# A scan's 32x32 block inverses put in place on chip instead of through DRAM, with weights and block inputs loaded earlier

## The chip, the cores and the metric

One core of a Trainium2 chip runs the whole program. The metric is the device time of one execution in microseconds, as the median over several runs. The engines are named as in the profile: PE (TensorE, matrix products), DVE (VectorE), ACT (ScalarE), POOL (GpSimd) and SP (SyncE, which here issues every DMA). Each works through its own instructions in order.

## What is computed

One trunk layer of a diffusion backbone over 1152 tokens (128 of context, 1024 latent) of width 1024: a SwiGLU block, a token mixer, a second SwiGLU block, each followed by a layer norm. The mixer projects its input once; one part feeds a bidirectional recurrence, one a pooling branch, one the gates that merge them:

```python
def _rwkv7_step(S, inp):
    r, w, k, v, kk, a = inp
    sa = jnp.einsum('dbhvk,dbhk->dbhv', S, kk)
    S = S * w[..., None, :] - sa[..., :, None] * (kk * a)[..., None, :] + v[..., :, None] * k[..., None, :]
    return S, jnp.einsum('dbhvk,dbhk->dbhv', S, r)
...
u = jnp.einsum('btgc,gcd->btgd', u, p['w_pool']).reshape(b, t, D_B) * p['pool_scale']
y_b = u @ p['w_o_pool']
gate_a = jax.nn.sigmoid(gate_logits[..., :D_MODEL])
gate_b = jax.nn.sigmoid(gate_logits[..., D_MODEL:])
return (gate_a * y_a + gate_b * y_b) @ p['w_out'], s_final
```

There are 16 heads of 64 and two directions.

## The kernel before

**Precision.** Every large product is made of three: a value is split into a high part (a cast) and a low part (the rest), and high x high, high x low, low x high are added in PSUM (`mm3`, lines 155 to 160). So each weight tile is loaded raw (`wr`), cast on ACT (`wh`) and subtracted on POOL or DVE (`wl`). `Weights` (lines 109 to 129) does this by tiles of 1024 columns, `Halves` (lines 131 to 153) by halves of 512 with four buffers of each kind, always with its subtraction on POOL.

**Stages**, in the profile's time: first SwiGLU block and projections up to about 1560 us; a gate phase (lines 888 to 894) in which eight columns of gate logits are computed for three blocks of 384 tokens, with the first two block inverses and the pooling sums beside it; the scan from 1676 us; its end, from 2325 to 2390 us, in which the last group norms are finished; then the output projections and the second SwiGLU block.

**The scan.** The recurrence goes by chunks of 64 tokens: 18 chunks for each of two halves of the heads, 36 steps, each for both directions and eight heads. `main(s)` (line 1090) multiplies the chunk's `ak` with the state (line 1109) and with the masked products `LM` (line 1115) into `xy`; ACT copies this to `Xs` (line 1119); a product with the inverse `W` of a triangular matrix gives `us` (line 1125), which ACT negates into `vu` (line 1128); this updates the state (lines 1135 to 1137) and gives the output `xy`, copied to `yt` (line 1145). Inside the scan all five engines take their instructions in the order in which the program writes them (line 1241).

**The inverses.** A `Solve` (line 749) makes the 64x64 inverses of two step pairs at once: 2 directions x 2 diagonal blocks of 32 x 32 matrices lie on 128 partitions, 32x32 elements each. `pairs` eliminates row after row on DVE (lines 772 to 779). The result `Wd` has the matrix on the partition and its row and column along it; the matmuls need the row (or column) on the partition. `out` therefore stores it to DRAM, `back` loads it in pieces of 32 elements into `Wb` and `Dx`, and `t0` and `t1` transpose 32x32 blocks on DVE. `ph1` and `ph2` then make the off-diagonal block on PE, with ACT copies between. The work of a solve is spread over 24 slots, three in each scan step (`at`, line 828): slot 0 is after the Xs copies, slot 1 after the vu copies, slot 2 at the end of a step. Solve i + 1 starts 12 slots after solve i, and its loads of `Gq` (line 765) are issued in the slot in which solve i stores `Wd`. There are nine solves; seven store their result in the scan.

**The filler.** Between the scan's products PE gets the remaining gate projections and the pooling branch (`filler`, line 956), one matmul at a time: for each of three blocks of tokens eight `proj` (24 matmuls each, two halves of weights), four pooling products and eight `back` (12 matmuls, one half). `fill` (line 1215) deals out 780 of some 900 of these over the 36 steps in the proportion 6 : 9 : 10 for the three slots. `Halves.get(i)` casts the halves up to i + 2 and has one more fetched. Blocks 1 and 2 read their inputs `hg` back from DRAM (line 1002); the pooled inputs `uf` are loaded by `load_u` (line 992) into two buffers.

**SP's queue** carries all of this in program order: chunk loads (line 867) three steps ahead, `vu` (line 875), the solve's loads and stores, weights (line 140), block inputs, and the stores collected by `later` and issued by `flush`.

Of the kernel before, what the change touches and what calls it, by code (L numbers as in the profile page):

```python
# [9 lines left out]
F32 = mybir.dt.float32  # L10
# [7 lines left out]
P = 128  # L18
# [43 lines left out]
def tile_step(ctx: ExitStack, tc: tile.TileContext, I: dict, O: dict):  # L62
# [68 lines left out]
    class Halves:  # L131
# [11 lines left out]
        def get(self, i, look=2):  # L143
            while len(self.got) < min(len(self.units), i + 1 + look):
                self.fetch(len(self.got) + 1)
                r = self.raws[len(self.got)]
                h = self.pool.tile([P, self.HW], F32R, name="wh", tag="wh", bufs=4)
                l = self.pool.tile([P, self.HW], F32R, name="wl", tag="wl", bufs=4)
                A.copy(h, r)  # L149
                G.tensor_tensor(l, r, h.bitcast(F32), ALU.subtract)  # L150
                self.got.append((h, l))
            self.fetch(len(self.got) + 1)
            return self.got[i]
# [443 lines left out]
    with pool("mp", 4, psum=True) as psum, pool("ma", 2, psum=True) as paux, \  # L597
# [151 lines left out]
        class Solve:  # L749
# [30 lines left out]

            def out(self):
                self.pairs(31)
                self.ed = dram.tile([2, 2, 32, 32, 32], F32, name="ed", tag="ed", bufs=2)
                S.dma_start(self.ed.rearrange("d b n i t -> (d b n) i t"), self.Wd)

            def back(self):
                W = self.W = Wb[self.i % 2]
                self.D = self.t4("Dx", "dx")
                self.N = self.t4("Nt", "nt")
                for b in range(2):  # L790
                    S.dma_start(W[32 * b:32 * b + 32, :, 32 * b:32 * b + 32], self.ed[0, b].rearrange("n i t -> i n t"))
                    S.dma_start(self.D[64 + 32 * b:96 + 32 * b], self.ed[1, b].rearrange("n i t -> i n t"))
                for k in range(2):
                    u = 2 * self.i + k
                    for d in range(2):
                        c0 = chunk0(u, d)
                        S.dma_start(self.N[64 * d:64 * d + 32, k * 16:k * 16 + 16].rearrange("s (a n) t -> s a (n t)", a=4),
                                    nd_d[d][u // 9][c0 // 6][:, :, c0 % 6:c0 % 6 + 2].rearrange("s a c e t -> s a (c e t)"))

            def t0(self):  # L800
                V.transpose(self.D[0:32], self.W[0:32, :, 0:32])

            def t1(self, b):
                r = slice(64 + 32 * b, 96 + 32 * b)
                V.transpose(self.W[r, :, 32 * b:32 * b + 32], self.D[r])

# [7 lines left out]
            def ph1(self, k):  # L814
                ks = slice(16 * k, 16 * k + 16)
                N, D, W = self.N, self.D, self.W
                pm = self.ph(lambda n: ((slice(32, 64), N[0:32, n, :], D[0:32, n, :]), (slice(96, 128), N[64:96, n, :], W[64:96, n, 0:32])), k)
                A.copy(N[32:64, ks], pm[32:64])
                A.copy(N[96:128, ks], pm[96:128])

            def ph2(self, k):
                ks = slice(16 * k, 16 * k + 16)
                N, D, W = self.N, self.D, self.W
                pm = self.ph(lambda n: ((slice(0, 32), N[32:64, n, :], W[32:64, n, 32:64]), (slice(96, 128), D[96:128, n, :], N[96:128, n, :])), k)
                A.mul(W[0:32, ks, 32:64], pm[0:32], -1.0)
                A.mul(W[96:128, ks, 0:32], pm[96:128], -1.0)

            def at(self, n):
# [6 lines left out]
                elif n == 12:  # L835
                    self.out()
                elif n == 14:
                    self.back()
                elif n == 16:
                    self.t0()  # L840
                elif n == 17:
                    self.t1(0)
                elif n == 18:
                    self.ph1(0)
                elif n == 19:
                    self.ph2(0)
                elif n == 20:
                    self.t1(1)
                    self.ph1(1)
                elif n == 21:  # L850
                    self.ph2(1)
# [26 lines left out]
        with pool("m2") as pl:  # L878
# [8 lines left out]
            load_v(1, 0, (2, 17))  # L887
            for n in range(EARLY):
                for b in (2, 1, 0):
                    ps = psum.tile([P, 512], F32, name="pm", tag="mm")  # L890
                    gemm(ps, W.get(27 + n), hs, b)
                    ga = s0.tile([P, 8, 64], F32, name="ga", tag="Xs", bufs=2).rearrange("p h v -> p (h v)")[:, :BN]
                    A.activation(ga, ps[:, :BN], AF.Sigmoid)  # L893
# [34 lines left out]
    for b in range(NB):  # L928
        gunits += [I["w_pool"].rearrange("p g c -> p (g c)"), *halves(mix[39])]
        for n in range(8):  # L930
            if n < 7:
                gunits += halves(mix[40 + n])
            gunits.append(halves(I["w_op"][n // 2])[n % 2])
# [22 lines left out]
    def filler(psG):  # L956
        u = 0

        def nextw(look=2):
            nonlocal u  # L960
            u += 1
            return GW.get(u - 1, look)

        for b in range(NB):
            sl = slice(b * BN, (b + 1) * BN)
            hh = hs[0]
            if b:
                hh = [hpA.tile([P, KT, BN], F32R, name="hg", tag="hb") for k in range(2)]
            if b:
# [28 lines left out]
            wp = nextw()  # L998
            if b:
                for ks in (slice(0, 4), slice(4, 8)):  # L1000
                    for k in range(2):
                        S.dma_start(hh[k][:, ks].bitcast(F32), h2_d[b][k][:, ks])
            first = chain(proj(0), proj(1))
            next(first)
            yield
            for g in range(4):
# [3 lines left out]
                G.tensor_tensor(ul, uf, uh.bitcast(F32), ALU.subtract)  # L1010
                if g < 2:
                    ufs.append(load_u(g + 2))
                for _ in range(PWGAP):
# [3 lines left out]
                yield from steps3(ps[:, :BN], [(w3(wp[0], g), w3(wp[1], g), uh, ul)])  # L1017
                t = sg.tile([P, BN], F32, name="ut", tag="ut")
                A.activation(t, ps[:, :BN], AF.Copy, scale=pcol("pool_scale", g))
                split(t, u2[0], u2[1], g, G)  # L1020
            yield from first
            yield from back(b, u2, gts, 0)
            for n in range(2, 8):
                yield from proj(n)
                if n < 7:
                    yield from back(b, u2, gts, n - 1)
            prev = (b, u2, gts)
# [3 lines left out]
    with pool("s1") as pl, pool("gn") as gn, pool("spa", 2, psum=True) as psA, pool("spx", 1, psum=True) as psX, \  # L1031
# [58 lines left out]
        def main(s):  # L1090
# [7 lines left out]
            LM, KBT = c["LM"].pop(s), c["KBT"].pop(s)  # L1098
            Xs = s0.tile([P, 8, 64], F32, name="Xs", tag="Xs", bufs=2)
            if s % 2 == 0:  # L1100
# [140 lines left out]
        with tc.manual_schedule(engines={PE.engine, V.engine, A.engine, G.engine, S.engine}):  # L1241
# [30 lines left out]
            while gns or waitgn:  # L1272
                if waitgn:
                    gns.append(waitgn.pop(0))
                for _ in range(2):
                    flush()
                    drive(gns)
                    for _ in range(8):
                        next(fl, None)
            for _ in fl:  # L1280
# [179 lines left out]
```

## Time and profile before

| | us |
|---|---|
| median of 3 runs | 3470.34 (3469.39 to 3471.6) |
| the profiled execution, its own time | 3476.58 |
| its span, first to last instruction | 3474.5 |
| PE busy over the span | 3236.0 (93%) |
| DVE busy | 1999.5 (58%) |
| POOL busy | 1311.7 (38%) |
| ACT busy | 1149.4 (33%) |

The profile is that of one execution. Busy shares are over the whole span, and the stages differ: a stage's own limit is read from its windows and from the waits inside it. "Clock" is the share of full speed that was granted to PE. A wait is the idle time of an engine ahead of an instruction, put down to what ended it. L1109 means line 1109 of the kernel before.

### The profile page before, as it was taken

The numbers are of one execution on the slowest core, as the hardware profiler recorded it, in microseconds if no ns is written. First come the engines' busy times: TensorE is split into PE (matmuls) and PEld (weight loads), VectorE is DVE, ScalarE is ACT, GpSimd is POOL, SyncE is SP. The second block draws the span as 40 slices with busy tenths as digits, with TensorE's granted clock in tenths as the row PEclk, the third lists the DMA queues.
The fourth block names the chain that finished last, engine by engine and source line by source line (L and its number), as shares of the span: only waits on it lengthen the run. The fifth ranks groups of instructions, "written<-read, shape, count | busy, mean of one in ns | idle before, by whom it ended". The sixth has DMA issues, their size and how long they took to land.

```text
span 3474.5 us, 62657 instructions
## 1 busy us (share of the span) xinstructions
PE 3236.0 (93%) x25742; PEld 3072.7 (88%) x25742; DVE 1999.5 (58%) x3309; ACT 1149.4 (33%) x1970; POOL 1311.7 (38%) x1026
## 2 busy tenths in 40 slices
PE   7999999999999999798899888988999999999997
PEld 7999999999988887587788777887999999999996
DVE  6888633347557788858476667544574332323466
ACT  4111111125434444431343444454345111111133
POOL 5111211136456666653221442257764111111144
PEclk9999999999999999698999889999999999999998
DMA  6344211124455545564455666656551111111133
GB/s 233 129 140 133 91 37 42 45 92 132 185 167 159 162 151 155 161 194 159 135 159 171 184 178 188 197 160 201 204 168 52 37 42 44 43 43 43 49 127 105
DMA packets 310270, 442.74 MB, mean 127 GB/s; under 512 B 115424, under 2 KB 211168, under 8 KB 308960
## 3 DMA queue, kind: packets, MB, share of 16 engines
q1 hardware_dynamic: 309984, 438.74, 39.8%
q8 instruction: 202, 3.31, 0.4%
q14 instruction: 84, 0.69, 0.1%
HBM read 316.01 MB, written 101.25 MB: 120 GB/s over the span
## 4 chain that ended last, share of the span: by engine, by line
PE 60%; DVE 14%; DMA 10%; issue 5%; POOL 5%; SPq 3%; ACT 3%; DVEq 0%; POOLq 0%; ACTq 0%
PE pg L159 8%; PE pg L160 8%; PE pg L158 8%; PE po L158 5%; PE po L159 5%; PE po L160 5%; PE pm L158 2%; PE pm L160 2%; PE pm L159 2%; PE pa L1078 2%; DVE wl L127 2%; PE xy L1109 2%; DMA fm<-in_w_mod 1%; DVE pr L776 1%; DVE Wd L778 1%
## 5 line engine op out<-in xcount | busy, mean ns | idle before, releaser
L125 ACT CAST wh<-wr 128x1024 fp32r<-128x1024 f32 x270 | 280.7, 1049 | 817.5 <-PE po L159 433.7
L127 POOL TENSOR_TENSOR wl<-wr,wh 128x1024 fp32r<-128x1024 f32 x117 | 291.4, 2490 | 505.7 <-ACT wh L125 473.7
L295 POOL TENSOR_TENSOR gl<-sg,gh 128x384 fp32r<-128x384 f32 x132 | 159.9, 1212 | 783.7 <-ACT gh L294 783.6
L158 PE MATMUL po<-gh,wh 128*128 128x384 f32 x1056 | 357.8, 339 | 6.7 <-DVE acc L312 3.3
L159 PE MATMUL pg<-h1l,wh 128*128 128x384 f32 x1056 | 356.6, 338 | 5.7 <-POOL h1l L167 5.6
L159 PE MATMUL po<-gl,wh 128*128 128x384 f32 x1056 | 357.2, 338 | 3.6 <-POOL gl L295 3.6
L160 PE MATMUL po<-gh,wl 128*128 128x384 f32 x1056 | 358.0, 339 | 0.0
L158 PE MATMUL pg<-h1h,wh 128*128 128x384 f32 x1056 | 357.6, 339 | 0.0
L160 PE MATMUL pg<-h1h,wl 128*128 128x384 f32 x1056 | 355.7, 337 | 0.0
L127 DVE TENSOR_TENSOR wl<-wr,wh 128x1024 fp32r<-128x1024 f32 x153 | 222.7, 1460 | 230.7 <-ACT wh L125 230.7
L158 PE MATMUL pg<-h3h,wh 128*128 128x384 f32 x1056 | 353.6, 336 | 0.0
L160 PE MATMUL pg<-h3h,wl 128*128 128x384 f32 x1056 | 353.3, 335 | 0.0
L159 PE MATMUL pg<-h3l,wh 128*128 128x384 f32 x1056 | 353.1, 335 | 0.0
L158 PE MATMUL pm<-h2h,wh 128*128 128x384 f32 x936 | 329.8, 352 | 12.6 <-ACT ga L893 11.7
L292 DVE TENSOR_TENSOR sg<-sg,pg 128x384 f32<-128x384 f32 x132 | 73.1, 553 | 460.3 <-PE pg L160 454.2
L160 PE MATMUL pm<-h2h,wl 128*128 128x384 f32 x936 | 328.8, 351 | 2.0 <-DVE wl L127 2.0
L159 PE MATMUL pm<-h2l,wh 128*128 128x384 f32 x936 | 328.4, 351 | 0.0
L312 DVE SCALAR_TENSOR_TENSOR ac<-po,modh,ac 128x384 f32<-128x384 f32 (+1 forms) x352 | 172.7, 514 | 96.9 <-PE po L160 96.9
L403 DVE SCALAR_TENSOR_TENSOR fm<-fm 128x512 f32<-128x512 f32 x224 | 182.8, 816 | 53.6 <-DMA fm<-in_w_mod 50.3
L150 POOL TENSOR_TENSOR wl<-wr,wh 128x512 fp32r<-128x512 f32 x75 | 98.5, 1316 | 303.9 <-ACT wh L149 223.8
L158 PEld LDWEIGHTS po<-gh,wh 128*128 128x128 f32 x1056 | 199.5, 189 | 9.6 <-PE po L160 3.6
L159 PEld LDWEIGHTS pg<-h1l,wh 128*128 128x128 f32 x1056 | 200.5, 190 | 8.1 <-POOL h1l L167 7.6
(285 smaller groups left out, 7565.3 us busy)
## 6 DMA issues: line engine op xcount, KB each, us to landing
wr<-in_ffn_in SPq DMA_DIRECT2D x120, 512.0 KB
ak<-ak SPq DMA_DIRECT2D x48, 768.0 KB
ak<-ak SPq DMA_DIRECT2D x72, 512.0 KB
wr<-in_ffn_out SPq DMA_DIRECT2D x60, 512.0 KB
fm<-in_w_mod SPq DMA_DIRECT2D x112, 256.0 KB
wr<-in_w_mix SPq DMA_DIRECT2D x39, 512.0 KB
sh<-pads SPq DMA_DIRECT2D x108, 130.0 KB
wr<-in_w_mix SPq DMA_DIRECT2D x48, 256.0 KB
```

The source lines that it names most:

```text
L125: A.copy(h[:, :w], r[:, :w])
L127: e.tensor_tensor(l[:, :w], r[:, :w], h[:, :w].bitcast(F32), ALU.subtract)
L150: G.tensor_tensor(l, r, h.bitcast(F32), ALU.subtract)
L158: PE.matmul(ps, wh, xh, start=first and k == 0, stop=False)
L159: PE.matmul(ps, wh, xl, start=False, stop=False)
L160: PE.matmul(ps, wl, xh, start=False, stop=last and k == n - 1)
L292: lastv[0] = V.tensor_tensor(sg, sg, pu[:, :BN], ALU.mult)
L295: G.tensor_tensor(gs[j, b][1][:, sl], sg, gs[j, b][0][:, sl].bitcast(F32), ALU.subtract)
L312: lastv[0] = V.scalar_tensor_tensor(accs[b][:, n, s0:s1], po[:, s0:s1], modh[:, gate_i // 4, n, g:g + 1], accs[b][:, n, s0:s1], ALU.mult, ...
L403: V.scalar_tensor_tensor(jk, w, 1.0, silc[:, s, hf * 512:hf * 512 + 512], ALU.mult, ALU.mult, accum_out=part[:, kt, s, hf:hf + 1])
L1078: PE.matmul(pa[e][:, i, :], ak[es, i, 128:256], ak[es, i, 0:128], start=True, stop=True)
L1109: PE.matmul(xy[:, e, d, i, :], ak[d][es, i, 0:128], states[q, d][es, i, :], start=(i == 0 and d == 0), stop=False, skip_group_check=True)
```

## The change

The solve keeps its result on chip: two DVE transposes over all 128 partitions make `X` (row on the partition) and `Y` (column on the partition), and four ACT copies (two per direction, in two slots) put the diagonal blocks into `W`. The products of `ph1` and `ph2` come one slot earlier for the first half. `Halves.get` fetches two halves beyond the cast ones instead of one. A block's inputs `hg` are loaded after the last projection of the block before, ahead of three `back` groups, and each `back` comes one projection later; the order of the weight halves follows. `uf` is scaled in place, and its buffer's next load follows the split. In the gate phase two weight columns go together, and block 0's products of both come last; its results have buffers of their own. In the end of the scan one drive of the group norms and ten filler matmuls make a round instead of two drives with eight each.

```diff
--- before.py
+++ after.py
@@ -149,7 +149,7 @@
                 A.copy(h, r)
                 G.tensor_tensor(l, r, h.bitcast(F32), ALU.subtract)
                 self.got.append((h, l))
-            self.fetch(len(self.got) + 1)
+            self.fetch(len(self.got) + 2)
             return self.got[i]
 
     def mm3(ps, pairs, first=True, last=True):
@@ -778,18 +778,16 @@
                     V.tensor_tensor(Wd[:, 0:k + 1, k + 1:32], Wd[:, 0:k + 1, k + 1:32], o, ALU.subtract)
                 self.k = min(31, self.k + n)
 
-            def out(self):
+            def swap(self):
                 self.pairs(31)
-                self.ed = dram.tile([2, 2, 32, 32, 32], F32, name="ed", tag="ed", bufs=2)
-                S.dma_start(self.ed.rearrange("d b n i t -> (d b n) i t"), self.Wd)
+                Wd = self.Wd
+                self.X = self.t4("Xi", "dx")
+                self.Y = self.t4("Yt", "yt")
+                V.transpose(self.X.rearrange("p n t -> p t n"), Wd.rearrange("p i t -> p t i"))
+                V.transpose(self.Y.rearrange("p n i -> p i n"), Wd)
 
             def back(self):
-                W = self.W = Wb[self.i % 2]
-                self.D = self.t4("Dx", "dx")
                 self.N = self.t4("Nt", "nt")
-                for b in range(2):
-                    S.dma_start(W[32 * b:32 * b + 32, :, 32 * b:32 * b + 32], self.ed[0, b].rearrange("n i t -> i n t"))
-                    S.dma_start(self.D[64 + 32 * b:96 + 32 * b], self.ed[1, b].rearrange("n i t -> i n t"))
                 for k in range(2):
                     u = 2 * self.i + k
                     for d in range(2):
@@ -797,12 +795,11 @@
                         S.dma_start(self.N[64 * d:64 * d + 32, k * 16:k * 16 + 16].rearrange("s (a n) t -> s a (n t)", a=4),
                                     nd_d[d][u // 9][c0 // 6][:, :, c0 % 6:c0 % 6 + 2].rearrange("s a c e t -> s a (c e t)"))
 
-            def t0(self):
-                V.transpose(self.D[0:32], self.W[0:32, :, 0:32])
-
-            def t1(self, b):
-                r = slice(64 + 32 * b, 96 + 32 * b)
-                V.transpose(self.W[r, :, 32 * b:32 * b + 32], self.D[r])
+            def place(self, d):
+                W = self.W = Wb[self.i % 2]
+                for b in range(2):
+                    r = slice(64 * d + 32 * b, 64 * d + 32 * b + 32)
+                    A.copy(W[r, :, 32 * b:32 * b + 32], (self.Y if d else self.X)[r])
 
             def ph(self, jobs, k):
                 pm = PPS[0].tile([P, 16, 32], F32, name="ph", tag=PPS[1])
@@ -813,15 +810,15 @@
 
             def ph1(self, k):
                 ks = slice(16 * k, 16 * k + 16)
-                N, D, W = self.N, self.D, self.W
-                pm = self.ph(lambda n: ((slice(32, 64), N[0:32, n, :], D[0:32, n, :]), (slice(96, 128), N[64:96, n, :], W[64:96, n, 0:32])), k)
+                N, W, Y = self.N, self.W, self.Y
+                pm = self.ph(lambda n: ((slice(32, 64), N[0:32, n, :], Y[0:32, n, :]), (slice(96, 128), N[64:96, n, :], W[64:96, n, 0:32])), k)
                 A.copy(N[32:64, ks], pm[32:64])
                 A.copy(N[96:128, ks], pm[96:128])
 
             def ph2(self, k):
                 ks = slice(16 * k, 16 * k + 16)
-                N, D, W = self.N, self.D, self.W
-                pm = self.ph(lambda n: ((slice(0, 32), N[32:64, n, :], W[32:64, n, 32:64]), (slice(96, 128), D[96:128, n, :], N[96:128, n, :])), k)
+                N, X, W = self.N, self.X, self.W
+                pm = self.ph(lambda n: ((slice(0, 32), N[32:64, n, :], W[32:64, n, 32:64]), (slice(96, 128), X[96:128, n, :], N[96:128, n, :])), k)
                 A.mul(W[0:32, ks, 32:64], pm[0:32], -1.0)
                 A.mul(W[96:128, ks, 0:32], pm[96:128], -1.0)
 
@@ -833,19 +830,17 @@
                 elif n < 12:
                     self.pairs((2, 1, 5)[n % 3])
                 elif n == 12:
-                    self.out()
-                elif n == 14:
+                    self.swap()
+                elif n == 13:
                     self.back()
-                elif n == 16:
-                    self.t0()
+                    self.place(0)
+                elif n == 15:
+                    self.place(1)
                 elif n == 17:
-                    self.t1(0)
+                    self.ph1(0)
                 elif n == 18:
-                    self.ph1(0)
-                elif n == 19:
                     self.ph2(0)
                 elif n == 20:
-                    self.t1(1)
                     self.ph1(1)
                 elif n == 21:
                     self.ph2(1)
@@ -885,11 +880,11 @@
                 load_ak(s_, cs_, 0)
             load_v(0, 0, (0, 1))
             load_v(1, 0, (2, 17))
-            for n in range(EARLY):
-                for b in (2, 1, 0):
+            for n0 in range(0, EARLY, 2):
+                for n, b in ((n0, 2), (n0, 1), (n0 + 1, 2), (n0 + 1, 1), (n0, 0), (n0 + 1, 0)):
                     ps = psum.tile([P, 512], F32, name="pm", tag="mm")
                     gemm(ps, W.get(27 + n), hs, b)
-                    ga = s0.tile([P, 8, 64], F32, name="ga", tag="Xs", bufs=2).rearrange("p h v -> p (h v)")[:, :BN]
+                    ga = pl.tile([P, 8, 64], F32, name="ga", tag="ga", bufs=2).rearrange("p h v -> p (h v)")[:, :BN]
                     A.activation(ga, ps[:, :BN], AF.Sigmoid)
                     S.dma_start(gab_d[n][b][:, 0, :], ga)
             for g, w in enumerate(WINDOWS):
@@ -927,9 +922,10 @@
 
     for b in range(NB):
         gunits += [I["w_pool"].rearrange("p g c -> p (g c)"), *halves(mix[39])]
+        gunits += halves(mix[40])
         for n in range(8):
-            if n < 7:
-                gunits += halves(mix[40 + n])
+            if n < 6:
+                gunits += halves(mix[41 + n])
             gunits.append(halves(I["w_op"][n // 2])[n % 2])
     BO = (1, 0, 2)
     GW = Halves(gctx.enter_context(pool("gw", side="right")), gunits)
@@ -961,11 +957,9 @@
             u += 1
             return GW.get(u - 1, look)
 
+        hh = hs[0]
         for b in range(NB):
             sl = slice(b * BN, (b + 1) * BN)
-            hh = hs[0]
-            if b:
-                hh = [hpA.tile([P, KT, BN], F32R, name="hg", tag="hb") for k in range(2)]
             if b:
                 for n in (6, 7):
                     yield from back(*prev, n)
@@ -996,10 +990,6 @@
 
             ufs = [load_u(0), load_u(1)]
             wp = nextw()
-            if b:
-                for ks in (slice(0, 4), slice(4, 8)):
-                    for k in range(2):
-                        S.dma_start(hh[k][:, ks].bitcast(F32), h2_d[b][k][:, ks])
             first = chain(proj(0), proj(1))
             next(first)
             yield
@@ -1008,22 +998,24 @@
                 uh, ul = [sg.tile([P, BN], F32R, name="us", tag=f"us{k}", bufs=1) for k in range(2)]
                 A.copy(uh, uf)
                 G.tensor_tensor(ul, uf, uh.bitcast(F32), ALU.subtract)
-                if g < 2:
-                    ufs.append(load_u(g + 2))
                 for _ in range(PWGAP):
                     next(first)
                     yield
                 ps = psG.tile([P, 512], F32, name="pw", tag="mm")
                 yield from steps3(ps[:, :BN], [(w3(wp[0], g), w3(wp[1], g), uh, ul)])
-                t = sg.tile([P, BN], F32, name="ut", tag="ut")
-                A.activation(t, ps[:, :BN], AF.Copy, scale=pcol("pool_scale", g))
-                split(t, u2[0], u2[1], g, G)
+                A.activation(uf, ps[:, :BN], AF.Copy, scale=pcol("pool_scale", g))
+                split(uf, u2[0], u2[1], g, G)
+                if g < 2:
+                    ufs.append(load_u(g + 2))
             yield from first
-            yield from back(b, u2, gts, 0)
             for n in range(2, 8):
                 yield from proj(n)
-                if n < 7:
-                    yield from back(b, u2, gts, n - 1)
+                if n == 7 and b < 2:
+                    hh = [hpA.tile([P, KT, BN], F32R, name="hg", tag="hb") for k in range(2)]
+                    for ks in (slice(0, 4), slice(4, 8)):
+                        for k in range(2):
+                            S.dma_start(hh[k][:, ks].bitcast(F32), h2_d[b + 1][k][:, ks])
+                yield from back(b, u2, gts, n - 2)
             prev = (b, u2, gts)
         for n in (6, 7):
             yield from back(*prev, n)
@@ -1096,7 +1088,7 @@
             vu = [vus[d][u % 2][:, m[d]] for d in range(2)]
             ak = aks.pop(s)
             LM, KBT = c["LM"].pop(s), c["KBT"].pop(s)
-            Xs = s0.tile([P, 8, 64], F32, name="Xs", tag="Xs", bufs=2)
+            Xs = s0.tile([P, 8, 64], F32, name="Xs", tag="Xs", bufs=1)
             if s % 2 == 0:
                 c["yt"] = pl.tile([P, 2, 8, 64], F32, name="yt", tag="yt", bufs=1)
             yt = c["yt"]
@@ -1272,11 +1264,10 @@
             while gns or waitgn:
                 if waitgn:
                     gns.append(waitgn.pop(0))
-                for _ in range(2):
-                    flush()
-                    drive(gns)
-                    for _ in range(8):
-                        next(fl, None)
+                flush()
+                drive(gns)
+                for _ in range(10):
+                    next(fl, None)
             for _ in fl:
                 pass
             flush()
```

## Rows read from the trace of the kernel before

**Rows 1.** Windows: busy us (instructions) of PE, PEld, DVE, ACT, POOL; clock; DMA. Last: L1109 alone.
```profile
1707.00:2261.00 554.00, 489.01 (x8689) 440.00 (x8690) 373.36 (x755) 247.97 (x458) 161.60 (x132) 0.91 0.61 178
...
2325.00:2390.00 65.00, 39.24 (x181) 34.96 (x179) 23.35 (x35) 24.17 (x49) 42.13 (x33) 0.82 0.61 195
...
1707.00:2261.00 554.00, 66.67 (x962) 62.33 (x964) 0.91 0.61 178
```

**Rows 2.** Windows, the same columns: the first of four steps without a stall; their sum.
```profile
2107.30:2125.20 17.90, 17.64 (x421) 16.05 (x420) 14.59 (x30) 11.07 (x21) 5.73 (x6) 1.00 0.57 173
...
sum 61.90, PE 61.55 PEld 55.67 DVE 49.20 ACT 31.30 POOL 14.72; mean PE 15.39 PEld 13.92 DVE 12.30 ACT 7.82 POOL 3.68
```

**Rows 3.** Waits of PE, 1676 to 2261 us: total us, times, longest.
```profile
PE us L1125 <- ACT Xs L1119: 15.3, 4, 7.9
...
PE pm L940 <- ACT wh L149: 12.9, 1, 12.9
...
PE pm L940 <- DMA hg<-h: 10.6, 2, 7.9
...
PE sp L1135 <- ACT vu L1128: 8.9, 2, 5.6
...
PE xy L1109 <- ACT yt L1145: 8.5, 2, 6.8
...
PE xy L1109 <- POOL Sc L1046: 4.3, 1, 4.3
...
PE pm L942 <- DMA hg<-h: 2.6, 2, 1.4
...
PE pm L940 <- ACT ut L1019: 1.3, 1, 1.3
```

**Rows 4.** Waits of ACT, the same stretch and columns.
```profile
ACT wh L149 <- DMA wr<-in_w_mix: 54.1, 8, 14.0
...
ACT wh L149 <- DMA wr<-in_w_op: 27.3, 7, 5.9
```

**Rows 5.** Timeline of SP's DMA issues, 1985 to 2030 us: start, us, what.
```profile
1991.08 7.71 SPq L765 DMA_DIRECT2D Gq<-qd  x8
...
2000.77 0.61 SPq L140 DMA_DIRECT2D wr<-in_w_mix  x1
```

**Rows 6.** Timeline of ACT and PE, same stretch; in brackets the idle time before.
```profile
2009.26 0.62 ACT L149 CAST wh<-wr 128x512 fp32r<-128x512 f32 x1 [14.03 <-DMA wr<-in_w_mix]
...
2010.26 1.18 ACT L1119 COPY Xs<-xy 64x512 f32<-64x512 f32 x2
...
2010.89 1.41 PE L1125 MATMUL us<-Xs,Wb 64*64 64x64 f32 x12 [7.87 <-ACT Xs L1119]
```

**Rows 7.** Solve's operations: ns min/median/max, first and last start us; page: DMA packets.
```profile
L791 SPq DMA_DIRECT2D Wb<-ed x18: 318/617/4921, 1596.4 to 2225.7; - x18
...
L792 SPq DMA_DIRECT2D Dx<-ed x18: 546/564/4314, 1596.8 to 2226.3; - x18
...
L805 DVE STREAM_TRANSPOSE Wb<-Dx x18: 1235/1239/1242, 1602.0 to 2259.1; 32x1024 f32<-32x1024 f32 x18
...
L825 ACT ACTIVATE Wb<-ph x18: 587/588/591, 1613.5 to 2266.2; 32x512 f32<-32x512 f32 x18
...
DMA packets 310270, 442.74 MB, mean 127 GB/s; under 512 B 115424, under 2 KB 211168, under 8 KB 308960
```

**Rows 8.** Timeline of DVE: first and last pair product of one solve.
```profile
1558.31 0.19 DVE L776 TENSOR_TENSOR pr<-Wd,Gq 128x31 f32<-128x31 f32 x1 [6.99 <-DMA Nt<-nd]
...
1592.10 0.23 DVE L778 TENSOR_TENSOR Wd<-Wd,pr 128x31 f32<-128x31 f32 x1
```

**Rows 9.** Waits of the SP queue, 1676 to 2261 us: total us, times, longest.
```profile
SPq L994 <- POOL us L1010: 26.3, 5, 10.7
```

**Rows 10.** Waits of PE in the gate phase, 1560 to 1676 us.
```profile
PE pm L158 <- ACT ga L893: 11.7, 1, 11.7
...
PE ph L811 <- DVE Dx L801: 4.9, 1, 4.9
```

## The prediction

> **What bounds the kernel now.** I read the busy table by stretch first, then TensorE's waits in the scan, then ScalarE's waits, and last the SP queue and ScalarE side by side in one bad stretch. [...] Four steps without a stall (one of them with the inverse's matmuls) take 61.9 us, 61.55 busy, the first at clock 1.00 [rows 2]. The stretch holds 962/32 = 30 steps [rows 1], so stall-free it would last 30/4 x 61.9 = 464 us. It lasts 554: 90 us too many, 65 idle and about 25 of work slowed by the clock, which falls after such idle times. TensorE itself therefore bounds the scan, wherever nothing interrupts it.
>
> TensorE's waits from step 0 on name the interrupters: ScalarE's copies Xs, vu and yt, with 15.3, 8.9 and 8.5 us, a memset of the state on POOL with 4.3, together 37.0; the block inputs `hg` from DRAM with 10.6 + 2.6 = 13.2; and 12.9 once, for the first weights of the filler [rows 3]. The small copies are not slow; they queue. In the same stretch ScalarE stood 54.1 + 27.3 us idle ahead of its weight casts of line 149, waiting for the weights to land [rows 4]. One stretch shows the whole chain: SP takes 7.7 us to issue the eight `Gq` loads of the next solve and issues a weight load only at 2000.77 [rows 5]; the cast comes at 2009.26 after 14.03 us of waiting; Xs sits behind it on the in-order ScalarE at 2010.26, and TensorE resumes at 2010.89 after 7.87 us [rows 6]. So late DMA, behind the solve's loads in one queue, becomes a TensorE stall.
>
> **The change part by part.**
>
> 1. **One more half of weights ahead.** Today a half is fetched one `get` before the one that casts it, then two. The filler hands out 780 matmuls over 36 steps, 21.7 a step; a half feeds 12. At 61.9/4 = 15.5 us a step [rows 2] a `get` comes every 8.6 us, so each load starts some 8.6 us sooner. Against a longest wait of 14.0 and a mean of 54.1/8 = 6.8 and 27.3/7 = 3.9 us [rows 4], that removes nearly all: beyond 8.6 us only 14.0 leaves more than a few. The extra raw half fits the four buffers: the one it overwrites was cast two `get`s before. I take 85% of the 37.0 us: -31.5. Bounds: 0 (SP as late as before) and -37.
>
> 2. **Block inputs sooner.** The four 768 KB loads go out before three `back` groups, 36 matmuls or 36/21.7 x 15.5 = 26 us sooner; TensorE waited 7.9 us at the longest [rows 3]. I take all 13.2. They now wait for the last projection of the block; what is queued behind them on SP are weights (with their new lead), chunk loads three steps ahead and stores, so nothing that TensorE wants at once.
>
> 3. **The way through DRAM goes.** Per solve this removes one store and four loads. SP issues two of each kind of load, medians 0.62 and 0.56 us, up to 4.9 when the queue is full [rows 7], some 3 to 7 us of queue time per solve. Those loads are 4 x 32 x 32 = 4096 pieces of 128 B per solve, 36,864 of the 115,424 packets under 512 B [rows 7]. The SP wait for `Wd` does not go: the next `Gq` load, right behind it, needs VectorE to be through with the same pairs. I count this as part of step 1's 85%, not again.
>
> 4. **VectorE.** Three transposes of 32x1024 go, 3 x 1.24 = 3.7 us [rows 7]; two of 128x1024 come, in one slot. The trace has none of 128 partitions, and none with the new access patterns, whose neighbouring elements lie 128 B apart. Nearest are the pair products: 31 elements in a row take 0.19 us, 31 single elements 128 B apart 0.23 [rows 8], some 1 ns more per element. From below a transpose costs today's 1.24; from above 1.24 + 1024 x 1 ns = 2.3. I take the upper for both, 4.6 a solve, 0.9 more than today, as rows 8 are nearest in their access pattern [rows 8]. [...] VectorE is busy 49.2 of 61.9 us in the clean steps [rows 2], so I charge nothing; if that cover fails, the state update behind the swap is late, then the next step's transposes of `ak`.
>
> 5. **ScalarE** gets four copies of 32x1024 per solve. A 32x512 pass takes 0.59 [rows 7], so at most 1.2 each, 4.7 a solve, 33 over the seven solves of this stretch. Two sit behind the vu copies, where TensorE has filler, state and output matmuls before it needs ScalarE again; two behind Xs, with filler and the us matmuls. ScalarE is busy 31.3 of 61.9 [rows 2]. Bounds 0 and +33; nearer to 0: I take +4.
>
> 6. **Pool inputs.** `load_u` moves behind the split, so SP waits longer there (today 26.3 us in five waits [rows 9]). The reordered projection and `back` have the same matmuls. Nothing in the sum; it is a rival.
>
> 7. **Gate phase, end.** Two stalls stand before the scan, 11.7 and 4.9 us [rows 10]. The second is the wait for a transpose behind the DRAM trip, but its successor may stand at the same place, and the weights of every second gate column now have one product instead of three in which to be converted. The 11.7 (a store queued on SP) stays. At the end TensorE is busy 39.2 of 65 us [rows 1], paced by POOL; one drive with ten steps instead of two with eight each leaves POOL's work as it was. Both 0, with -17 to +10 as bounds together. The first 12.9 also stays: the first weights are queued behind the same loads.
>
> 8. **Clock.** The addressed idle time is 31.5 + 13.2 = 44.7 of 65; of the 25 us of slow work I give back the same share, -17.
>
> **Sum:** -31.5 - 13.2 - 17 + 4 = -58 us. The profiled execution took 3476.6 us (span 3474.5), 6.2 above the median of 3470.3; the forecast is 3476.6 - 58 = 3418.6 there and **3412** as median. A measurement of this kernel can tell about 0.2%, 7 us.
>
> **Rivals.**
> - *The next limit takes half.* With the weights in time, the copies of step 5 fall on the path (+33 instead of +4): -29, 3441. For it: Xs, vu and yt each hold a step's chain, and they were the longest waits [rows 3]. Against it: ScalarE is half idle in clean steps.
> - *More than forecast.* All 50.2 us of stalls and their 19 of clock go, and the 11.7 + 4.9 of the gate phase [rows 10] with them: -86, 3384. Against it: nothing in the diff moves the first of these.
> - *The lookahead does nothing.* SP itself is late, so a load emitted earlier is still issued behind the same `Gq` loads (7.7 us in a row [rows 5]). Only `hg` and its clock are saved: -18, 3452.
> - *Slower: SP stands still.* Six `load_u` now wait for TensorE, ScalarE twice and POOL in turn, two `hg` groups for a projection. At the longest wait of today, 10.7 us in the same line [rows 9], eight of them cost 86; were all of it TensorE's, -58 + 86 = +28, 3498. It decides from 58/8 = 7.3 us each. Against it: the mean is 26.3/5 = 5.3 [rows 9], and of TensorE's waits only 1.3 us led to this chain [rows 3].
>
> **How the numbers follow.** Forecast (gain of 40 to 80) 0.62; more than that 0.10; half or less 0.15; no change 0.05; slower 0.08. The range 3388 to 3455 holds the forecast, the bounds of its terms and the smaller gains, and leaves out most of "more", "no change" and "slower". Faster 0.87, same 0.05, slower 0.08.
>
> **What would show it.** Right: line 149's waits for weights fall from 81 us in that stretch to under 20, TensorE's waits for `hg` vanish, steps 1 to 30 last under 500 us at a clock of 0.97 or more, packets under 512 B fall by 37 thousand, transposes take 1.2 to 2.3 us. Wrong: line 149 still waits, or Xs and vu wait with the casts in time (step 5), or SP's line 994 waits over 60 us (the slower rival), or the stretch shrinks and the gate phase or the end grows by as much.

## The result, and the profile after

The changed kernel takes 3419.53 us (median of 4 runs, 3412.68 to 3426.26) against 3469.86 us: a ratio of 0.9861, 95% interval 0.9833 to 0.9889, 50 us by the medians. The forecast was 3412, a gain of 58, with a range of 3388 to 3455. The profiled execution took 3418.87 us, where the sum had 3418.6.

The windows of the changed kernel, in the columns of [rows 1]: the gate phase, steps 1 to 30 of the scan, and its end.

```profile
1560.00:1674.00 114.00, 94.65 (x756) 90.95 (x756) 79.52 (x132) 24.67 (x41) 33.65 (x23) 0.88 0.37 128
...
1704.60:2210.80 506.20, 465.09 (x8688) 418.42 (x8687) 372.33 (x743) 280.01 (x488) 162.07 (x131) 0.97 0.58 180
...
2275.00:2334.00 59.00, 39.97 (x179) 35.56 (x178) 23.00 (x33) 24.06 (x49) 43.11 (x33) 0.82 0.65 205
```

The reader is to see that 48 us of the 57.7 between the two profiled executions lie in one stretch, steps 1 to 30 of the scan, 554 to 506 us, with as many products as before. The idle time there fell by 24 us, from 65 to 41; the busy time fell by 24 us too, from 489 to 465, as the granted clock rose from 0.91 to 0.97. The end gave 6 us, the gate phase about 2. The forecast had steps 1 to 30 under 500 us; that was not reached.

What TensorE waited for in the scan (total us, times, longest), to be held against [rows 3] and this line of the same view of the kernel before:

```profile
PE pt L1086 <- DVE Sc L1136: 5.4, 4, 4.2
```

The changed kernel:

```profile
PE pt L1078 <- DVE Sc L1128: 14.5, 11, 2.9
PE pm L936 <- ACT wh L149: 12.8, 1, 12.8
PE sp L1127 <- ACT vu L1120: 11.7, 5, 6.3
PE pw L936 <- DVE gt L983: 6.2, 1, 6.2
PE pb L936 <- DVE gt L983: 3.8, 1, 3.8
PE xy L1101 <- POOL Sc L1038: 2.2, 1, 2.2
```

The waits for `hg`, Xs and yt are gone. VectorE has taken their place: the state update Sc and the gated sums gt, 24.5 us together. The wait for vu did not fall but rose, from 8.9 to 11.7 us. Of ScalarE's 81.4 us of waiting for weights [rows 4] nothing is left, but for the one wait for the first weights:

```profile
ACT wh L149 <- DMA wr<-in_w_pool: 11.4, 1, 11.4
```

The new operations (ns min/median/max), and the page's count of packets, to be held against [rows 7]:

```profile
L786 DVE STREAM_TRANSPOSE Xi<-Wd x9: 2021/2175/2193, 1591.1 to 2172.4; 128x1024 f32<-128x1024 f32 x9
...
L787 DVE STREAM_TRANSPOSE Yt<-Wd x9: 1866/1921/1961, 1593.2 to 2174.5; 128x1024 f32<-128x1024 f32 x9
...
L802 ACT COPY Wb<-Xi x18: 1044/1045/1047, 1593.4 to 2175.7; 32x1024 f32<-32x1024 f32 x18
...
DMA packets 271533, 433.29 MB, mean 127 GB/s; under 512 B 77840, under 2 KB 173584, under 8 KB 270224
```

The transposes take 2.18 and 1.92 us, near the upper bound of 2.3; small packets fell by 37,584.

VectorE's own waits for DMA ahead of line 776, the first pair product of a solve, are still there: 40 us in five groups over steps 1 to 30. The two largest:

```profile
DVE pr L776 <- DMA bb<-bon: 11.7, 1, 11.7
DVE pr L776 <- DMA wr<-in_w_mix: 10.6, 2, 6.1
```

### The profile page after: what moved, and what is told of

Same layout as the page of the kernel before. It is cut to its first block, busy times and chain, and to the rows that moved or that the text cites. A ratio compares the mean times of both kernels' runs of the same rounds, so it can differ in the third digit from the quotient of the medians.

```text
span 3416.8 us, 62644 instructions
## 1 busy us (share of the span) xinstructions
PE 3206.2 (94%) x25742; PEld 3044.4 (89%) x25742; DVE 2002.7 (59%) x3300; ACT 1187.2 (35%) x2006; POOL 1308.0 (38%) x1026
## 4 chain that ended last, share of the span: by engine, by line
PE 60%; DVE 16%; DMA 9%; issue 5%; POOL 5%; ACT 3%; SPq 2%; DVEq 0%; POOLq 0%; ACTq 0%
PE pg L159 9%; PE pg L160 9%; PE pg L158 9%; PE po L159 4%; PE po L158 4%; PE po L160 4%; PE pm L158 2%; PE pm L160 2%; PE pm L159 2%; DVE wl L127 2%; PE pa L1070 2%; PE xy L1101 2%; DVE Wd L778 2%; DVE fm L403 2%; DVE pr L776 2%
## 5 line engine op out<-in xcount | busy, mean ns | idle before, releaser
L160 PE MATMUL pm<-h2h,wl 128*128 128x384 f32 x936 | 328.2, 351 | 16.7 <-DVE wl L127 16.7
L160 PEld LDWEIGHTS pm<-h2h,wl 128*128 128x128 f32 x936 | 182.1, 195 | 24.0 <-DVE wl L127 17.3
```

The source lines that it names most:

```text
L160: PE.matmul(ps, wl, xh, start=False, stop=last and k == n - 1)
```

## The experiments

Theory A is the prediction's: weights that land late stall ScalarE, and through it TensorE. Theory B makes the trip of `Wd` through DRAM the cause, however early the weights are asked for. The first four runs add one part to the kernel before, or take one from the changed kernel. Where a run is held against another one than the kernel before, the difference is that of the two medians; the ratios, each against the kernel before measured beside it, give up to 5 us more or less, and are added where that matters.

**Lookahead alone**, on the kernel before.

```diff
-            self.fetch(len(self.got) + 1)
+            self.fetch(len(self.got) + 2)
             return self.got[i]
```

> The kernel before with the lookahead of two halves and nothing else. Theory A (weights that land late stall ScalarE, and through it TensorE): most of the weight part of the gain, 30 to 45 us faster than before (about 3430 us), ScalarE's waits for weights in line 149 from 112 us in the whole run to under 35. Theory B (the trip through DRAM crowds the queue, and weights are late because of it however early they are asked for): under 12 us faster, line 149 still waits over 70 us.

Measured: 3457.15 us, ratio 0.9977 (0.9956 to 0.9998): 8 us by the ratio. ScalarE's waits in line 149 did what A says, over the whole run:

```profile
ACT wh L149 <- DMA wr<-in_w_pool: 10.5, 1, 10.5
...
ACT wh L149 <- DMA wr<-in_w_mix: 3.0, 2, 2.5
```

From 112 us to 13.5, and yet the time hardly moved: A is right on the waits, B on the time. In steps 1 to 30 TensorE is idle 68 us, no less than before; what this stretch gained came with the clock, 0.94 against 0.91:

```profile
1701.00:2241.50 540.50, 472.69 (x8690) 425.32 (x8688) 373.21 (x755) 248.52 (x457) 161.48 (x131) 0.94 0.63 183
```

The waits for Xs and yt are gone. TensorE's waits from step 1 to 2240 us show what came instead:

```profile
PE pt L1086 <- DVE Sc L1136: 21.5, 7, 6.5
PE pm L940 <- DMA hg<-h: 17.7, 1, 17.7
PE sp L1135 <- ACT vu L1128: 15.4, 2, 9.2
```

The state update on VectorE, with 5.4 us a small row before, is the longest now. One stretch of this kernel shows why, first SP's issues in the timeline (start, us, what):

```profile
1983.92 0.42 SPq L784 DMA_DIRECT2D ed<-Wd  x1
1984.40 7.10 SPq L765 DMA_DIRECT2D Gq<-qd  x8
...
1992.02 0.43 SPq L769 DMA_DIRECT2D Wd<-in_id  x1
```

and VectorE's timeline, with the idle time before an instruction in brackets:

```profile
1998.83 1.26 DVE L776 TENSOR_TENSOR pr<-Wd,Gq 128x31 f32<-128x31 f32 x1 [13.70 <-DMA Wd<-in_id]
...
2010.22 0.41 DVE L1136 TENSOR_TENSOR Sc<-Sc,sp 128x256 f32<-128x256 f32 x1
```

The next solve's `Wd` starts as unit matrices loaded over the old `Wd` (line 769). In SP's queue this load stands behind the store of the old `Wd` and the eight `Gq` loads. VectorE, in order, stands 13.7 us before the first pair product, and the state update of the step stands behind the pairs. Five of TensorE's seven waits for it, 20.4 of the 21.5 us, end 8 to 12 us after such a stand of VectorE has ended.

**On-chip turn alone**, on the kernel before, with what makes room for it.

```diff
-            def out(self): ...
+            def swap(self): ...
-                Xs = s0.tile([P, 8, 64], F32, name="Xs", tag="Xs", bufs=2)
+                Xs = s0.tile([P, 8, 64], F32, name="Xs", tag="Xs", bufs=1)
```

> The kernel before with the transposes and copies on chip, and with what makes room for them (one Xs buffer, pooled inputs scaled in place, gate results in buffers of their own), but with the old lookahead, the old loads of hg, the old order of gate columns and the old end. Theory A: 3 to 15 us faster than before. Theory B: 30 us or more, and line 149's waits for weights fall from 112 us to under 50.

Measured: 3434.95 us, ratio 0.9906 (0.9878 to 0.9933), 33 us by the ratio: theory B in time. Line 149 still waited 72 us, where B had under 50, so B's "because of it" holds only in part.

**Changed kernel without the lookahead.** The edit of the first run, reversed.

> The changed kernel with the old lookahead of one half. Theory A: 25 to 40 us of the gain are lost (about 3450 us), line 149 waits over 70 us for weights. Theory B: under 10 us are lost (about 3425 us).

Measured: 3434.87 us, ratio 0.9906 (0.9881 to 0.9931): 15 us lost, between the two. Line 149 waited 79 us; so the same wait seems to cost more once the trip through DRAM is gone than before, 15 against 8, but the intervals of the two overlap, and this is not shown.

**Changed kernel through DRAM.**

```diff
-            def swap(self): ...
-            def place(self, d): ...
+            def out(self): ...
+            def t0(self): ...
+            def t1(self, b): ...
```

> The changed kernel with the old way of the blocks through DRAM (store, four loads, three transposes of 32 partitions; the old slots). Theory A: 3 to 15 us lost (3422 to 3435 us), with under 30 us of waits for weights in line 149. Theory B: 30 us or more lost (3450 us or more).

Measured: 3450.12 us, ratio 0.9946 (0.9924 to 0.9968): 31 us lost, theory B's number, with 17 us of waits in line 149 as theory A wants it. Late weights were thus one symptom of the queue, and by these medians no more than a third of the gain. VectorE's waits for DMA in this kernel (1700 to 2240 us) are another, 51 us against the 40 of the changed kernel:

```profile
DVE pr L776 <- DMA Wb<-ed: 20.7, 2, 15.0
...
DVE pr L776 <- DMA Wd<-in_id: 12.3, 1, 12.3
DVE pr L776 <- DMA wr<-in_w_mix: 10.9, 1, 10.9
DVE pr L776 <- DMA bb<-bon: 6.7, 1, 6.7
```

All these stand ahead of one and the same line, the first pair product of a solve; the names are those of the transfer that landed last. The next run tests this by taking the unit matrices off the queue.

**Through DRAM, unit matrices on chip** (the run above, with two memsets on POOL).

```diff
-                S.dma_start(self.Wd, I["id32"])
+                G.memset(self.Wd, 0.0)
+                G.memset(self.Wd.rearrange("p i t -> p (i t)")[:, 0:1024:33], 1.0)
```

> The changed kernel with the old way through DRAM, but with the unit matrices made by memsets on POOL: the next solve's start value now waits for the store of the last one alone, not for a load queued behind it. Measured so far: the way through DRAM costs about 30 us (3450 against 3419.5), the load of the unit matrices about 12 without it. If the 30 us are in the main VectorE waiting for that load at the end of the queue: 20 us or more faster than through DRAM with the load (3430 us or less). If they are the queue and the transfers themselves (SP's issue time, small pieces, loads of other work behind them): 5 to 15 us faster, no more than without the trip (3435 to 3445 us).

Measured: 3429.12 us, ratio 0.9895 (0.9879 to 0.9911): 21 us faster than with the load by the medians, 18 by the ratios: about the bound of the first branch. But that branch's reading, that the trip's cost is in the main the wait for this load, does not follow, for the load costs something without the trip too: the same two memsets take 12 us off the changed kernel (below). Putting the trip back costs 31 us with the load and 22 without it (3429 against 3407), so only some 9 of the 31 us hang on the load behind the trip, and the intervals of the four ratios together are wider than that. VectorE still waits 34 us ahead of the pairs here, the largest:

```profile
DVE pr L777 <- DMA y<-y: 11.7, 1, 11.7
DVE pr L777 <- DMA wr<-in_w_mix: 8.4, 1, 8.4
DVE pr L777 <- DMA gab<-gt: 7.2, 1, 7.2
```

**Block inputs late**: the changed kernel with the loads of `hg` where they were.

```diff
+            if b:
+                hh = [hpA.tile([P, KT, BN], F32R, name="hg", tag="hb") for k in range(2)]
...
-                if n == 7 and b < 2:
```

> The changed kernel with the block inputs hg loaded where they were before, behind the first pool inputs of their own block. Step 2 of the prediction: TensorE waits 10 to 20 us for hg again and the time grows by 13 to 20 us (3433 to 3440 us). Rival (the loads are hidden by the shorter queue since the trip through DRAM is gone): under 5 us.

Measured: 3433.35 us, ratio 0.9912 (0.9892 to 0.9931): 14 us lost. TensorE's waits:

```profile
PE pm L936 <- DMA hg<-h: 12.1, 2, 8.9
...
PE pm L938 <- DMA hg<-h: 2.3, 2, 1.2
```

By the ratios it is 18. Step 2 holds: 14.4 us of waits, where the prediction had 13.2 and its share of the clock (5 us).

**ScalarE's copies twice.**

```diff
-                    A.copy(W[r, :, 32 * b:32 * b + 32], (self.Y if d else self.X)[r])
+                    for _ in range(2):
+                        A.copy(W[r, :, 32 * b:32 * b + 32], (self.Y if d else self.X)[r])
```

> The changed kernel with each of the four ScalarE copies of a solve made twice: 4 x 1.04 = 4.2 us more of ScalarE per solve, 38 in all. Step 5 of the prediction (the copies lie beside other work): 0 to 8 us slower. Rival (ScalarE holds the chain of a step): 20 us or more.

Measured: 3428.57 us, ratio 0.9896 (0.9881 to 0.991): 9 us slower by the medians, 12 by the ratios, for 38 us more of ScalarE. Outside the step's bound of 8 and short of the rival's 20: most of the copies are covered, a quarter to a third is not. It shows at vu, 18.1 us where the changed kernel has 11.7:

```profile
PE sp L1128 <- ACT vu L1121: 18.1, 6, 6.6
```

**Transposes twice.**

```diff
-                V.transpose(...)  # both
+                for _ in range(2):
+                    V.transpose(...)  # both
```

> The changed kernel with both transposes made twice: 2.2 + 1.9 = 4.1 us more of VectorE per solve, 37 in all, in the slot of the swap. Step 4 of the prediction (covered by TensorE's work): 0 to 8 us slower. Rival (VectorE holds the state update behind the swap, so TensorE's waits for Sc grow): 20 us or more, waits for Sc from 14 to over 35 us.

Measured: 3445.13 us, ratio 0.9948 (0.9931 to 0.9964): 26 us slower for 37 us more of VectorE (30 by the ratios): the rival. TensorE's waits for the state update doubled, from 14.5 us, though they stayed below the rival's 35:

```profile
PE pt L1079 <- DVE Sc L1129: 30.0, 7, 6.1
```

**Unit matrices on chip**, in the changed kernel (the two memsets above).

> The changed kernel with the start value of Wd (32x32 unit matrices, 512 KB from DRAM per solve) made by two memsets on POOL. Theory C (what stalls TensorE now is VectorE, whose first pair products of a solve wait for this load in the crowded queue, 40 us in the scan, with the state update queued behind them): VectorE's waits for DMA ahead of line 776 fall under 10 us, TensorE's idle time in steps 1 to 30 from 41 to under 25 us, 10 to 25 us faster than the changed kernel (3395 to 3410 us). Theory D (the pairs wait for their Gq load just as long, or POOL's memsets of about 1 us delay the low halves): within 4 us of it.

Measured: 3407.36 us, ratio 0.9837 (0.9822 to 0.9851), 12 us below the changed kernel by the medians, 8 by the ratios; the two intervals overlap. By the medians within theory C's range of time, by the ratios just short of it. Its rows fell less than it said: VectorE still waits 17 us ahead of the pairs, for `Gq` and what lands with it:

```profile
DVE pr L777 <- DMA Nt<-nd: 15.8, 4, 8.2
...
DVE pr L777 <- DMA gab<-gt: 1.3, 1, 1.3
```

and TensorE is busy 467.81 of 500.60 us in steps 1 to 30, 33 us idle where C wanted under 25. C names the larger part of VectorE's waits (40 to 17 us), D the rest.

This kernel and the one through DRAM with the unit matrices on chip differ by the trip and what takes its place. Their steps 1 to 30, the one through DRAM first:

```profile
1700.80:2222.20 521.40, 476.27 (x8689) 427.58 (x8688) 375.96 (x754) 247.94 (x458) 166.50 (x142) 0.94 0.62 183
1702.60:2203.20 500.60, 467.81 (x8688) 421.21 (x8687) 369.49 (x743) 279.53 (x488) 167.77 (x143) 0.97 0.58 176
```

Of the 20.8 us between them 12.3 are idle time of TensorE and 8.5 the same products at a lower clock. TensorE's waits differ most at one pooling product, which stands behind ScalarE's cast of a pooled input (the same order):

```profile
PE pw L942 <- ACT us L1005: 13.0, 1, 13.0
...
PE pw L937 <- ACT us L1000: 4.5, 1, 4.5
```

SP's timeline in the kernel through DRAM shows what is issued ahead of that input's load:

```profile
1897.94 0.32 SPq L792 DMA_DIRECT2D Wb<-ed  x1
...
1902.62 0.56 SPq L793 DMA_DIRECT2D Dx<-ed  x1
...
1907.38 1.52 SPq L994 DMA_DIRECT2D uf<-u  x2
```

The four loads of pieces take up 5.2 us of SP's queue here, and the input's load goes out 12.1 us after the eight `Gq` loads are issued, against 7.7 without the trip. So the trip's own place in the queue explains part of this one wait; the rest of its cost is not taken apart.

**Transposes in two slots**: the second one behind the vu copies, in the kernel of the last run.

```diff
-                V.transpose(self.Y.rearrange("p n i -> p i n"), Wd)
...
             def back(self):
+                V.transpose(self.Y.rearrange("p n i -> p i n"), self.Wd)
```

> The kernel with the unit matrices made on chip, with the second transpose one slot later (behind the vu copies). Doubled transposes cost 26 us, so VectorE's 4.1 us in one slot are not covered. If it is their standing together ahead of the state update that costs: 5 to 15 us faster than 3407 us, TensorE's waits for Sc under 6 us. If it is VectorE's work as such in the step: within 4 us of 3407.

Measured: 3408.29 us, ratio 0.9831 (0.9812 to 0.985): no change, the second branch: that the two stand side by side costs nothing that could be seen. Both still stand ahead of the same step's state update, so the run does not tell what they would cost behind it.

**Low halves of the gate phase on POOL.** In the changed kernel's gate phase TensorE waits for them behind VectorE's pairs:

```profile
PE pm L160 <- DVE wl L127: 16.7, 2, 9.1
PE ph L808 <- DVE Yt L787: 2.0, 1, 2.0
```

```diff
+            W.eng = "p"
             for n0 in range(0, EARLY, 2):
```

> The kernel with the unit matrices made on chip, with the low halves of the gate phase's weights on POOL alone instead of POOL and VectorE in turn. In the changed kernel's gate phase TensorE waits 7.5 + 9.2 us for low halves that VectorE makes behind the pair products. If that order is the cause: 8 to 16 us faster than 3407 us, no such wait. If the next stall takes its place (gate results waiting for their stores): within 4 us of 3407.

Measured: 3396.96 us, ratio 0.9797 (0.9778 to 0.9817), 10 us below the run with the unit matrices on chip alone, where these waits were 13.3 us, and 6.5 for the gate results whose buffers wait for their stores. They became 2.5 and 5.0, so the order of VectorE's work was the cause:

```profile
PE pm L158 <- ACT ga L890: 5.0, 1, 5.0
PE ph L809 <- DVE Yt L788: 3.1, 1, 3.1
PE pm L160 <- POOL wl L127: 2.5, 1, 2.5
```

**First weights early**, on top of that.

```diff
+            GW.fetch(4)
             for s in range(n):
```

> The kernel of the run before (unit matrices on chip, gate low halves on POOL) with the filler's first four halves of weights issued on SP ahead of step 0 instead of behind its eight Gq loads. The wait of 12.8 us for the first weights has stood unchanged in every kernel so far. If SP's order is its cause: that wait falls under 4 us and the kernel is 8 to 16 us faster than 3397 us (3381 to 3389). If the halves have to wait for the room of the gate phase's tiles, or their transfers take as long from step 0: within 4 us of 3397.

Measured: 3394.37 us, ratio 0.9795 (0.9774 to 0.9816). The wait of 12.8 us is gone from step 0:

```profile
PE pw L938 <- ACT us L1001: 2.4, 1, 2.4
PE pm L942 <- POOL wl L150: 1.4, 1, 1.4
PE pm L938 <- ACT wh L149: 1.3, 1, 1.3
```

but the time is that of the second branch, within the interval of the run before. SP's order caused the wait; what it is worth stays open, at some few us. This is the fastest version measured by its median, 25 us below the changed kernel and about 2% faster than the kernel before.

## Why the prediction was right or wrong

The direction was right and the time near: 50 us by the medians against 58, and -57.7 us between the two profiled executions against a sum of -58. The place was right for 48 of these 57.7 us; the sum had all of them in steps 1 to 30. The sum was not right for its reasons.

- **Step 1 failed**, the largest term (-31.5 and its share of the clock). The lookahead alone gives 8 us, and taking it from the changed kernel costs 15. Its mechanism worked to the letter: the waits in line 149 went. The error was to read a wait that ends last as the only one. Behind the late weights stood VectorE, waiting for the same queue, and when the weights came in time TensorE stopped at the state update instead (5.4 us before, 21.5 with the lookahead alone). The sign was there: I read TensorE's and ScalarE's waits only, and VectorE's in the kernel before (1707 to 2261 us) have 48 us of DMA ahead of the same line 776, in these and three smaller groups:

```profile
DVE pr L776 <- DMA yn<-yo: 15.5, 1, 15.5
DVE pr L776 <- DMA Wd<-in_id: 11.9, 1, 11.9
```

- **Step 3 failed** in "I count this as part of step 1's 85%". The trip through DRAM is the main term: 31 us when put back into the changed kernel, 33 when taken from the kernel before. I priced its issue time and its packets, but not what stands behind it in SP's queue. That its longest issues met a full queue no view shows; the two of 4.9 us fell where the DMA share was 1.07 and 0.92. The load of the next unit matrices is one such, and the step's own remark that the wait for `Wd` does not go stopped at `Gq`, one load too early. That load costs 21 us with the trip and 12 without, so it explains some 9 of the 31; for the other 22 the runs show one place, the load of a pooled input.
- **Step 2 held**: 13.2 us plus 5 of clock against 14 by the medians, 18 by the ratios.
- **Step 4** had the durations (2.18 and 1.92 against an upper bound of 2.3), from the rows of single elements 128 B apart [rows 8]. "I charge nothing" was wrong as a statement on cover: VectorE is not covered, 37 us more of it cost 26. It did no harm that shows, as the transposes replace 3.7 us a solve by 4.1: with the old ones, through DRAM, TensorE waits 21.2 us for the state update, against 14.5. The transpose that reads and writes elements 128 B apart took 2.18 us, the one that only writes them so 1.92; what makes the difference was not shown.
- **Step 5** was small, though not as small as said: 38 us more cost 9 to 12, and the wait for vu, one of the signs of being wrong, rose from 8.9 to 11.7.
- **Step 7**: the gate phase came out near 0 by exchange. The low halves that must now be ready within one product did become a stall, 16.7 us, in place of the 11.7 and 4.9 [rows 10]. The end gave 6 us where the step had 0, inside its bounds.
- **Step 8** was too small beside its stalls. Steps 1, 2 and 5 had 31.5 + 13.2 - 4 = 40.7 us less idle time, and it fell by 24; step 8 had 17 us from the clock, and the busy time of the same products fell by 24 as the clock went from 0.91 to 0.97. That the clock falls after a stall shows in the kernel before: TensorE stood from 2003.0 to 2010.9 us [rows 6], and the granted clock was 1.00 up to 2008 us, 0.50 from 2010 to 2014 and 1.00 again from 2016 to 2018. Some 10 us more came outside the stretch, where the sum had none.
- **The rivals.** "The next limit takes half" was right in kind, since a next limit did take over, but that was VectorE and not the copies of step 5. "The lookahead does nothing" was near in time for its part but not in its reason, for the weights did come in time, and wrong in the total, since the trip through DRAM paid instead. "Slower" did not occur: SP waited 23.7 us in the line of `load_u`, against 26.3 [rows 9].

Two errors cancelled: of the weight term, 43 us with its share of the clock, 8 to 15 were real, and the trip through DRAM, counted at nothing of its own, was worth some 30. What the parts cost when taken out one at a time, 15, 31 and 14 us, adds up to more than the 50 gained, so they overlap. That the two profiled executions fitted to a microsecond is chance.

What stays open: the rest of the cost of the trip through DRAM, 22 us with the unit matrices on chip in both (3429 against 3407). One wait for a pooled input is 8.5 us of it, and SP's issue time stands ahead of that; SP's issue time elsewhere and the small packets were not separated.

## What to carry to other kernels

When several engines wait for one queue, the wait that ends last can hide the next one: here line 149's waits went from 112 to 13.5 us, and the time fell by 8. Before a term is priced, list what each engine, not the bound one alone, is waiting for at the same moment. When a transfer is removed, follow what is queued behind it and who starts on that: here taking out a load of constants that nobody counted gave 12 and 21 us in two kernels, as much as the weights (8 and 15). A constant that is loaded once per round over a buffer in use may be cheaper made on chip: here two memsets on POOL, 0.95 and 0.16 us a round, did it.

## What was not expected of the hardware

One full-width transpose of 128x1024 takes 1.92 us when it reads neighbouring elements and writes them 128 B apart, 2.18 when it also reads them so, against 1.24 for 32x1024 of today's pattern. An ACT copy of 32x1024 took 1.04 us, less than twice the 0.59 of 32x512. And the medians of one kernel moved by 5 us between groups of runs (3464.6 to 3469.9 for the kernel before), which is why the small differences above are given with the intervals of their ratios.
